# The last layer's second FFN product: its last six input tiles as Strassen blocks in two parts, with low parts made by accumulating transfers

## The chip, the cores and the metric

The kernel runs on one core of a Trainium2 chip. The metric is the device time of one execution in microseconds (us); the figure given for a kernel is the median of its runs.

## The reference, cut to what matters

A two-layer diffusion backbone over 1024 tokens of width 1024, with a 256-token context. The change is in the second product of the second layer's ConvFFN (D_FF = 2816, which is 22 input tiles of 128), which is followed only by the final norm:

```python
def conv_ffn(h, w_up, conv_w, conv_b, w_down, conv_fn):
    g, v = jnp.split(h @ w_up, 2, axis=-1)
    return (jax.nn.silu(conv_fn(g, conv_w, conv_b)) * v) @ w_down
...
        x = x + (gf * conv_ffn(hl, f_w_up[l], f_conv_w[l], f_conv_b[l], f_w_down[l], latent_hconv)).astype(x.dtype)
...
    return rms_norm(x, final_g)
```

## The kernel before

Every fp32 product is made of three fp32r matmuls: an operand is split into a high part (a rounded copy, made by ScalarE, `split`, line 231) and a low part (the operand minus its high part), and `mm` (line 444) adds high·low, low·high and high·high. The low part is made in one of two ways: VectorE subtracts (`split`), or ScalarE writes minus the high part and a DMA that GpSimd issues adds the operand to it from DRAM (`split_dma`, line 238).

`Plan` (line 57) records every operation; `flush` (line 121) sorts them by a list scheduler with costs and due times into one fixed order for each engine. So every instruction has line 165 in the profile. `lag` (line 117) is the delay that the scheduler assumes between engines. SP issues the ordinary DMAs in one queue, in the order of the plan.

`run_units` (line 377) plans the loads. Loads land in four tiles of 128x1024 (`raw`: raw_95, raw_96, raw_97 and raw3) or, for some inputs, in stage tiles (`s`). A landing tile takes its next load when its last reader is done. Weights live in eight slots of 128x512 (`wh`/`wl`, and `wh1`/`wl1`), inputs in 28 slots of 128x512 (`bh0`/`bl0` and `bh`/`bl`).

`ffn` (line 1163) makes gate and value tiles pair by pair. `v_post` (line 1182) multiplies them. For the first 16 of 22 tiles `store_blocks` (line 1200) makes the four input combinations of Strassen's scheme in Winograd's form on VectorE (four subtractions of 128x512) and stores operands and combinations to `bd` (one transfer of 256 KB and three of 512 KB for a pair); the last six are stored plainly to `ad`.

`down` (line 1228) multiplies by `w_down`. The first 16 input tiles come in two groups of eight. A group takes the eight output tiles as four pairs (q = 0 to 3) and makes for each pair seven products (numbered 1 to 7) over 512 columns, each with four input tiles, so 12 matmuls (`down_blocks`, line 1284); each product is added to `x` by VectorE (`scalar_tensor_tensor`, called an evict below). The last six input tiles are plain, in three pieces of columns, 0:512, 512:768 and 768:1024; a piece has eight output tiles of 18 matmuls each. After the evict of each, `residual` (line 1095) squares it on ScalarE and adds the squares into `acct` on VectorE (`norm_sq`, line 462). `final` (line 1371) turns a finished piece's sums into reciprocal roots, spreads them by a matmul, multiplies and stores the output; for pieces 0 and 1 this lies beside the next piece.

Of the kernel before, what the change touches and what calls it, by code (L numbers as in the profile page):

```python
# [13 lines left out]
P = 128  # L14
# [37 lines left out]
class Plan:  # L52
# [131 lines left out]
def hybrid_kernel(ctx: ExitStack, tc: tile.TileContext, out, xs, cs, c, cc, ada, vecs,  # L184
# [88 lines left out]
    bd = dp.tile([P, 7, KD, HALF], F32, tag="bd", name="bd")  # L273
# [32 lines left out]
    def wsrc(key):  # L306
        kind = key[0]
        if kind in ("x", "xc"):
            return wx[key[1]]
        if kind == "g":  # L310
            return wg[key[1]]
        if kind == "o":
            return wo[key[1]]
        if kind == "ri":
            return wri[key[1]]
        if kind == "bo":
            return wbo[key[1]]
        return wdn[key[1], key[2], :, 2 * D:]
# [12 lines left out]
    def weight_item(key):  # L331
        src = wsrc(key)
        n = src.shape[-1]

        def prep(sl, raws):
            hi, lo = flat(sl[0][0], sl[0][2], len(sl))[:, :n], flat(sl[0][1], sl[0][2], len(sl))[:, :n]
            split(hi, lo, raws[0].tile[:, :n], weight_hi[0])
            return hi, lo
        return Item(key, [Raw(src)], -(-n // HALF), prep)

# [121 lines left out]
    def norm_sq(s, m):  # L462
        n = s.stop - s.start
        if m == 0:
            accs[s.start] = acct[:, s.start // HALF, s.start % HALF:s.start % HALF + n]
            act(accs[s.start], x[:, m, s], AF.Square)
        else:
            q = tmp(n)
            act(q, x[:, m, s], AF.Square)
            if s.start >= 768 and m == KD - 1:  # L470
                accs["end"] = q
            else:
                add(accs[s.start], q, accs[s.start], V)
# [621 lines left out]
    def residual(l, sl, m, s, ps, keep):  # L1095
        stt(x[:, m, s], ps, gcol(l, sl, m), x[:, m, s])
        if keep:
            nc.sync.dma_start(xd[:, m, s], x[:, m, s])
        norm_sq(s, m)
# [63 lines left out]
    def ffn(l, second, i):  # L1163
# [18 lines left out]
        def v_post(j0):  # L1182
            done = {0: 0, 1: 0}

            def post(row, h, a, b):
# [7 lines left out]
                if j0 < 16:  # L1193
# [27 lines left out]
    def act_item(key, src, load_after, slots, after, pool="raw"):  # L1221

        def prep(sl, rs):
            for j in (0, 1):
                split(*bslot(slots[j]), rs[0].tile[:, j * HALF:(j + 1) * HALF])
        items[key] = Item(key, [Raw(src, load_after, pool)], 0, prep, after)

    def down(l, ends, i):
# [5 lines left out]
        for g in range(2):  # L1234
# [8 lines left out]
            for q in range(4):  # L1243
                steps = down_blocks(l, g, q, role)
                ends = [unit(f, *(acts[p] if q == 0 else []), k) for p, f, k in steps]
        R = released()
# [5 lines left out]
        last, second = i is None, None  # L1252
        if not last:
            begin, first, second = block_norm(i, R[12:] + R[:12])
        pieces = [H[0], slice(HALF, 768), slice(768, SEQ)] if last else H
        for z, s in enumerate(pieces):
            h, o = s.start // HALF, s.start % HALF
            for m in range(KD):
                def f(w, m=m, h=h, o=o, s=s):
# [5 lines left out]
                    residual(l, 5, m, s, ps, not last)  # L1265
                acts = [("act", l, "t", h, kk) for kk in range(3)] if m == 0 and o == 0 else []
                unit(f, *acts, ("dt", l, m, z))
                if z and last and m == 1:
                    fin = final(pieces[z - 1])
                    call(fin[0])  # L1270
                elif z and last and m == 3:
                    call(fin[1])
                elif z and not last:
                    if m == 0:
                        call(begin)
                    if m == 1:
                        call(norm_cols, i, 1, 0, 1, "norm_mix_g")
                        call(first)
        if last:
            for f in final(pieces[-1]):  # L1280
                call(f)
        return second
# [170 lines left out]
```

## Time and profile before

| | us |
|---|---|
| median of 3 runs | 2081.2 |
| lowest, highest run | 2079.53, 2084.16 |
| profiled execution | 2079.64 |
| its span | 2077.8 |
| VectorE busy in the span | 1640.3 |
| ScalarE busy in the span | 1175.6 |

The profiled execution's own time is 1.84 us above its span and 1.6 us below the median. The stretches of interest: the layer's products with the up weights end near 1850; the last group of Strassen products of `w_down` ends near 1998; the last six input tiles run from there to 2068; the final norm of the last piece follows.

### The profile page before, as it was taken

How to read it: one execution, taken by the hardware profiler on the slowest of the kernel's cores; microseconds unless marked ns; L12 is line 12 of the kernel's file. 1: busy time of each engine (PE TensorE's matmuls, PEld its weight loads, DVE VectorE, ACT ScalarE, POOL GpSimd, SP SyncE). 2: the span in 40 equal slices, each digit the busy share in tenths (PEclk: the TensorE clock that was granted, in tenths of full speed). 3: DMA queues.
4: the chain of work that ended last, by engine and by line, in shares of the span. 5: the costliest groups of instructions: out<-in, count | busy, mean ns of one | idle time of the engine just before them, and what ended most of it. 6: DMA issues, size and time to landing. Idle time of an engine off the chain costs nothing.

```text
span 2077.8 us, 25555 instructions
## 1 busy us (share of the span) xinstructions
PE 2032.1 (98%) x9218; PEld 1679.4 (81%) x9218; DVE 1640.3 (79%) x2408; ACT 1175.6 (57%) x1790; POOL 188.3 (9%) x220
## 2 busy tenths in 40 slices
PE   8899988999999999999999999999999999999998
PEld 6688877788888888878888888888888888878888
DVE  7998999879877787677578977857987776587767
ACT  6266878556655555646356544536655555574445
POOL 0000000010111111111001111001111111111100
PEclk9999999999999999999999999999999999999999
DMA  8644222673677777777465578754566665696655
GB/s 302 192 170 152 71 82 86 205 195 78 174 205 183 191 206 216 204 231 213 117 192 123 155 213 243 229 183 117 136 191 170 185 152 142 168 277 181 157 151 164
DMA packets 134527, 363.72 MB, mean 175 GB/s; under 512 B 13825, under 2 KB 18177, under 8 KB 134273
## 3 DMA queue, kind: packets, MB, share of 16 engines
q1 hardware_dynamic: 103296, 305.46, 44.0%
q0 software_dynamic: 31104, 56.64, 16.7%
q8 instruction: 72, 1.18, 0.2%
q14 instruction: 55, 0.44, 0.1%
HBM read 305.42 MB, written 56.62 MB: 174 GB/s over the span
## 4 chain that ended last, share of the span: by engine, by line
PE 80%; DVE 10%; ACT 4%; DMA 4%; issue 1%; SPq 0%; DVEq 0%; ACTq 0%
PE banks L165 80%; DVE mx L165 2%; ACT mx L165 2%; DMA s<-bd 2%; DVE bl L165 2%; DVE u L165 2%; DVE x L165 2%; DVE wl L165 1%; DMA raw<-in_wdn 1%; ACT bh L165 1%; ACT L165 1%; DVE ul L165 0%; DVE acct L165 0%; DMA x<-in_xs 0%; DVE s L165 0%
## 5 line engine op out<-in xcount | busy, mean ns | idle before, releaser
L165 PE MATMUL banks<-bh,wh 128*128 128x512 f32 (+1 forms) x2720 | 1055.0, 388 | 5.9 <-DVE x L165 2.0
L165 PE MATMUL banks<-bl,wh 128*128 128x512 f32 (+1 forms) x2720 | 1051.2, 386 | 8.8 <-DVE bl L165 8.5
L165 PE MATMUL banks<-bh,wl 128*128 128x512 f32 (+1 forms) x2720 | 1050.5, 386 | 2.1 <-DVE wl L165 2.1
L165 PEld LDWEIGHTS banks<-bl,wh 128*128 128x128 f32 x2720 | 511.8, 188 | 118.7 <-DVE bl L165 15.5
L165 PEld LDWEIGHTS banks<-bh,wh 128*128 128x128 f32 x2720 | 511.7, 188 | 114.5 <-ACT wh L165 3.9
L165 PEld LDWEIGHTS banks<-bh,wl 128*128 128x128 f32 x2720 | 511.6, 188 | 106.4 <-DVE wl L165 4.7
L165 ACT ACTIVATE wh<-raw 128x512 fp32r<-128x512 f32 (+2 forms) x386 | 275.3, 716 | 420.7 <-PE banks L165 369.2
L165 DVE SCALAR_TENSOR_TENSOR x<-banks,mod,x 128x512 f32<-128x512 f32 (+1 forms) x184 | 132.6, 726 | 127.0 <-PE banks L165 126.0
L165 POOL DMA_DIRECT2D wl<-in_wup x132 | 115.0, 871 | 1251.2 <-ACT wl L165 1188.5
L165 ACT ACTIVATE wh<-s 128x512 fp32r<-128x512 f32 x216 | 135.3, 628 | 99.2 <-DVE s L165 70.4
L165 ACT ACTIVATE s<-banks 128x512 f32<-128x512 f32 x174 | 103.5, 596 | 153.9 <-PE banks L165 149.9
L165 DVE TENSOR_TENSOR wl<-raw,wh 128x512 fp32r<-128x512 f32 (+2 forms) x170 | 157.8, 932 | 38.6 <-ACT wh L165 37.2
L165 DVE TENSOR_TENSOR wl<-s,wh 128x512 fp32r<-128x512 f32 x216 | 148.2, 688 | 44.0 <-ACT wh L165 41.5
L165 ACT ACTIVATE wl<-wh 128x512 fp32r<-128x512 f32 x216 | 136.1, 630 | 5.8
L165 DVE TENSOR_TENSOR s<-s,banks 128x512 f32<-128x512 f32 x158 | 107.9, 684 | 31.0 <-PE banks L165 30.6
L165 DVE SCALAR_TENSOR_TENSOR x<-s,vec,x 128x504 f32<-128x504 f32 x132 | 96.6, 741 | 23.4 <-ACT x L165 22.2
L165 DVE TENSOR_TENSOR s<-raw 128x512 f32<-128x512 f32 x72 | 49.6, 689 | 65.0 <-DMA raw<-in_wup 41.9
L165 DVE SCALAR_TENSOR_TENSOR acct<-acct,cb 128x1024 f32<-128x1024 f32 x69 | 84.1, 1219 | 2.1 <-DMA acct<-in_ada 2.1
L165 PE MATMUL banks<-uh,wh 128*128 128x512 f32 (+1 forms) x192 | 70.5, 367 | 8.2 <-ACT mx L165 6.7
L165 PE MATMUL banks<-ul,wh 128*128 128x512 f32 (+1 forms) x192 | 70.1, 365 | 3.1 <-DVE ul L165 3.1
L165 ACT ACTIVATE bh<-s 128x512 fp32r<-128x512 f32 x88 | 51.3, 623 | 37.5 <-DMA s<-bd 33.7
L165 DVE TENSOR_TENSOR bl<-s,bh 128x512 fp32r<-128x512 f32 x88 | 57.3, 687 | 16.1 <-ACT bh L165 16.0
(158 smaller groups left out, 1898.4 us busy)
## 6 DMA issues: line engine op xcount, KB each, us to landing
raw<-in_wup SPq DMA_DIRECT2D x92, 512.0 KB, 4.9
acct<-in_ada SPq DMA_DIRECT2D x69, 512.0 KB, 4.0
wl<-in_wup POOLq DMA_DIRECT2D x132, 256.0 KB, 5.7
bd<-x SPq DMA_DIRECT2D x48, 512.0 KB, 5.3
s<-bd SPq DMA_DIRECT2D x44, 512.0 KB, 5.2
raw<-in_wdn SPq DMA_DIRECT2D x32, 512.0 KB, 5.6
raw<-in_wdn SPq DMA_DIRECT2D x40, 384.0 KB, 3.5
raw<-in_wbi SPq DMA_DIRECT2D x26, 512.0 KB, 5.1
```

Of the source, the lines that this page charges most:

```text
L165: getattr(getattr(self.tc.nc, e), op)(*a, **k)
```

## The change

For the last layer alone, the last six input tiles are made by the same seven products, now over three input tiles each (9 matmuls instead of 12). Layer 0 keeps the plain form (`down_rest`, the old code moved).

- `v_post` also calls `store_blocks` for the last six tiles of the last layer: 12 more subtractions of 128x512 on VectorE, and stores to `bd` instead of `ad`.
- `last_group` makes 20 units of 512 columns (a unit is product and output pair: "10" is product 1 of pair 0) and then, in two pieces of 256 columns, products 5 and 3 of each pair: 8 units of 256 columns each. That is 180 matmuls of 512 columns and 144 of 256, where there were 144 and 288.
- The inputs' low parts (21 tiles) and the low parts of weights 1, 2 and 4 are made by `split_dma`; those of weight products 5, 6, 7 and 3 are made on VectorE from sums and differences of 128x384 (`late_items`). Weights of products 5 and 3 are loaded a second time: 16 loads of 128x768 where there were 24.
- Evicts: one for each product, 20 of 512 columns and 16 of 256 (before, 8 and 16).
- The scheduler's assumed delay after a GpSimd transfer goes from 3.0 to 5.0.

```diff
-        return 0.0 if a == b else 0.95 if a == "sync" else 3.0 if a == "gpsimd" else 1.9 if b == "sync" else 0.2
+        return 0.0 if a == b else 0.95 if a == "sync" else 5.0 if a == "gpsimd" else 1.9 if b == "sync" else 0.2
...
-    bd = dp.tile([P, 7, KD, HALF], F32, tag="bd", name="bd")
+    bd = dp.tile([P, 7, KFF // 2, HALF], F32, tag="bd", name="bd")
...
+    def late_items(name, src1, src2):
+        w = src1.shape[-1] // 2
+        raws = [[Raw(src1), Raw(src2)] for _ in range(2)]
...
+                t = {j: raws[p in (5, 3)][j].tile for j in need[p]}
...
+                if p in (5, 6):
+                    src = s[0] = stmp("w", w)
+                    add(src, a21, a22)
+                    if p == 6:
+                        sub(src, src, a11)
+                elif p == 7:
+                    src = a21
+                    sub(src, a11, a21)
+                elif p == 3:
+                    src = s[0]
+                    sub(src, src, a11)
+                    sub(src, a12, src)
+                else:
+                    split_dma(hi, lo, *{1: (a11, src1[:, :w]), 2: (a12, src1[:, w:]), 4: (a22, src2[:, w:])}[p])
+                    return hi, lo
+                split(hi, lo, src)
...
-                if j0 < 16:
+                if j0 < 16 or l:
...
+                if dma:
+                    split_dma(*bslot(i), t, src[:, j] if len(slots) > 1 else src)
+                else:
+                    split(*bslot(i), t)
...
+    def last_group(l, ends, stored, last_up):
+        role = roles[0]
+        rel = [(j, ends[t]) for t, (_, n) in enumerate(ROLES) for j in role[n]]
+        role3, acts, need = {}, {}, dict(ROLES)
+        for t, p in enumerate((1, 2, 6, 7, 4, 5, 3)):
+            at = rel[3 * t:3 * t + 3]
...
+                act_item(acts[p][e], src, last_up if t < 2 else ends[0] - 8, [j for j, _ in sl], sl[-1][1],
+                         "s" if t < 2 else "raw", True)
...
+        def step(p, q, s):
+            def f(w):
+                n, o = s.stop - s.start, s.start % HALF
+                if p in (1, 5):
+                    st[q, p] = bank()
+                ps = st[q, 5 if p in (3, 5) else 1][:, H[p == 2]][:, :n]
+                for k in range(3):
...
+                r, h = to[p]
+                t = s if p in (5, 3) else H[h]
+                stt(x[:, 2 * q + r, t], ps, gcol(l, 5, 2 * q + r), x[:, 2 * q + r, t])
+                if p in (2, 4, 5, 3):
+                    end(2 * q + r, t)
...
+        for pq in "10 20 60 11 70 21 40 61 12 71 13 41 62 63 72 73 22 23 42 43".split():
+            put(int(pq[0]), int(pq[1]), H[0])
+        pieces = [slice(HALF, 768), slice(768, SEQ)]
+        for z, s in enumerate(pieces):
+            for n, (p, q) in enumerate(((5, 0), (5, 1), (3, 0), (3, 1), (5, 2), (5, 3), (3, 2), (3, 3))):
+                put(p, q, s)
+                if n == 2:
+                    fin = final(pieces[z - 1] if z else H[0])
                     call(fin[0])
...
+                elif n == 4:
+                    call(fin[1])
```

**VectorE, first of the last stage.** These are the rows of the kernel before around the first evicts of the second piece; `x<-banks,mod,x` is an evict, `wl` the low part of a weight, `s<-eye,rt` and `x<-x,banks` the final norm of the piece ahead.

```order
L165 SCALAR_TENSOR_TENSOR x_85<-banks_72,mod_78,x_85 128x256
L165 TENSOR_TENSOR wl_94<-raw_97,wh_93 128x768
L165 SCALAR_TENSOR_TENSOR x_85<-banks_72,mod_78,x_85 128x256
L165 TENSOR_TENSOR wl_94<-raw3_2695,wh_93 128x768
L165 RECIPROCAL rt_84<-rt_84 128x4
L165 TENSOR_TENSOR s_2696<-eye_82,rt_84 128x512
```

One low part or the start of the norm stands between evicts. The changed kernel there, from the second evict of 256 columns (product 5 of pair 1) to the third (product 3 of pair 0); `s` of 128x384 are the weight sums.

```order
L165 SCALAR_TENSOR_TENSOR x_85<-banks_72,mod_78,x_85 128x256
L165 TENSOR_TENSOR wl1_2694<-s_2696,wh1_2693 128x384
L165 TENSOR_TENSOR wl_94<-s_2696,wh_93 128x384
L165 TENSOR_TENSOR s_2696<-raw3_2695 128x384
L165 TENSOR_TENSOR s_2696<-s_2696,raw_95 128x384
L165 RECIPROCAL rt_84<-rt_84 128x4
L165 TENSOR_TENSOR s_2696<-eye_82,rt_84 128x512
L165 TENSOR_TENSOR s_2696<-raw_95,s_2696 128x384
L165 TENSOR_TENSOR wl_94<-s_2696,wh_93 128x384
L165 TENSOR_TENSOR x_85<-x_85,banks_72 128x2x512 x2
L165 SCALAR_TENSOR_TENSOR x_85<-banks_72,mod_78,x_85 128x256
```

Ten operations, two of them 1024 columns wide, now stand between two evicts where one low part stood.

**VectorE, in the 512-column stage.** The kernel before, four evicts after the last group's end (`bl` is the low part of an input):

```order
L165 SCALAR_TENSOR_TENSOR x_85<-banks_72,mod_78,x_85 128x512
L165 TENSOR_TENSOR wl_94<-raw3_2695,wh_93 128x768
L165 SCALAR_TENSOR_TENSOR x_85<-banks_72,mod_78,x_85 128x512
L165 TENSOR_TENSOR wl_94<-raw_95,wh_93 128x768
L165 TENSOR_TENSOR acct_73<-s_2696,acct_73 128x512
L165 TENSOR_TENSOR bl_2692<-raw3_2695,bh_2691 128x512
```

Each evict waits for at most one low part ahead of it. The changed kernel, from the evicts of units 20 and 60 over those of 11, 70 and 21 (the three single ones):

```order
L165 SCALAR_TENSOR_TENSOR x_85<-banks_72,mod_78,x_85 128x512 x2
L165 TENSOR_TENSOR s_2696<-raw_97 128x384
L165 TENSOR_TENSOR s_2696<-s_2696,raw_95 128x384
L165 SCALAR_TENSOR_TENSOR x_85<-banks_72,mod_78,x_85 128x512
L165 TENSOR_TENSOR raw_97<-raw_95,raw_97 128x384
L165 SCALAR_TENSOR_TENSOR x_85<-banks_72,mod_78,x_85 128x512
L165 TENSOR_TENSOR wl1_2694<-s_2696,wh1_2693 128x384
L165 TENSOR_TENSOR wl_94<-raw_97,wh_93 128x384
L165 SCALAR_TENSOR_TENSOR x_85<-banks_72,mod_78,x_85 128x512
L165 TENSOR_TENSOR s_2696<-raw_95 128x384
```

The weight sum of unit 61, which reads raw_97, now stands ahead of the evicts of 11 and 70.

**SP, the landing tiles of that stage.** The kernel before, after its last weights of the Strassen groups:

```order
L165 DMA raw_96<-ad_91 128x2x512
L165 DMA raw_95<-ad_91 128x2x512
L165 DMA raw_97<-ad_91 128x2x512
L165 DMA raw3_2695<-in_wdn 128x768
L165 DMA raw_95<-in_wdn 128x768
L165 DMA raw3_2695<-in_wdn 128x768
L165 DMA raw_96<-in_wdn 128x768
L165 DMA raw_97<-in_wdn 128x768
```

The loads go round the four tiles. The changed kernel in the same place:

```order
L165 DMA raw_97<-bd_92 128x512
L165 DMA raw3_2695<-in_wdn 128x768
L165 DMA s_2696<-bd_92 128x512
L165 DMA raw_97<-bd_92 128x1024
L165 DMA raw_95<-in_wdn 128x768
L165 DMA raw_96<-bd_92 128x512
L165 DMA raw_97<-bd_92 128x512
L165 DMA raw_97<-bd_92 128x1024
L165 DMA raw_96<-in_wdn 128x768
L165 DMA raw_97<-in_wdn 128x768
```

raw_97 takes four loads of inputs one after another, and then the weights that unit 61 needs.

## Rows read from the trace of the kernel before

**Rows 1.** Page, part 1: busy us, share of span, instructions.

```profile
PE 2032.1 (98%) x9218; PEld 1679.4 (81%) x9218; DVE 1640.3 (79%) x2408; ACT 1175.6 (57%) x1790; POOL 188.3 (9%) x220
```

**Rows 2.** Chain of waits, 1940:2078: start us, us, what (xcount).

```profile
1939.81 128.26 PE banks L165 x706
```

**Rows 3.** Stretches: us, then PE, PEld, DVE, ACT, POOL busy; PEclk, DMA share, GB/s.

```profile
1998.30:2031.00 32.70, 32.70 (x147) 27.09 (x146) 20.54 (x29) 18.58 (x28) 0.00 (x0) 1.00 0.46 134
2031.00:2068.00 37.00, 37.00 (x306) 36.47 (x304) 31.41 (x53) 24.35 (x46) 0.00 (x0) 1.00 0.56 178
```

**Rows 4.** Timeline of PE: start us, us, operation, shapes, xcount.

```profile
2010.16 0.39 PE L165 MATMUL banks<-bh,wl 128*128 128x512 f32 x1
2010.39 0.39 PE L165 MATMUL banks<-bh,wh 128*128 128x512 f32 x1
...
2035.10 0.95 PE L165 MATMUL banks<-ones,acct 128*128 128x1 f32 x8
...
2040.29 1.02 PE L165 MATMUL banks<-s,ones 128*128 128x512 f32 x2
...
2062.13 0.28 PE L165 MATMUL banks<-bh,wh 128*128 128x256 f32 x1
2062.25 0.28 PE L165 MATMUL banks<-bl,wh 128*128 128x256 f32 x1
```

**Rows 5.** Timeline of DVE, the last 70 us; in brackets idle before, and its releaser.

```profile
1998.35 0.75 DVE L165 SCALAR_TENSOR_TENSOR x<-banks,mod,x 128x512 f32<-128x512 f32 x1 [1.97 <-PE banks L165]
...
2047.74 0.48 DVE L165 SCALAR_TENSOR_TENSOR x<-banks,mod,x 128x256 f32<-128x256 f32 x1
2048.14 0.42 DVE L165 TENSOR_TENSOR acct<-s,acct 128x256 f32<-128x256 f32 x1
...
2068.09 0.48 DVE L165 SCALAR_TENSOR_TENSOR x<-banks,mod,x 128x256 f32<-128x256 f32 x1 [0.76 <-PE banks L165]
```

**Rows 6.** Groups by line and form, 1998.3:2068: busy us, mean ns, idle before.

```profile
L165 DVE TENSOR_TENSOR acct<-s,acct 128x256 f32<-128x256 f32 x13 | 5.5, 420 | 0.7 <-ACT s L165 0.3
...
L165 DVE TENSOR_TENSOR x<-x,banks 128x1024 f32<-128x1024 f32 x4 | 4.8, 1215 | 0.0
...
L165 ACT ACTIVATE bh<-raw 128x512 fp32r<-128x512 f32 x6 | 3.4, 615 | 0.0
```

**Rows 7.** DMA issues, 1960:2070: KB each, median us from issue to landing.

```profile
raw<-in_wdn SPq DMA_DIRECT2D x24, 384.0 KB, 3.5
raw<-ad SPq DMA_DIRECT2D x4, 512.0 KB, 3.8
```

**Rows 8.** DMA issues, 1700:1960.

```profile
raw<-bd SPq DMA_DIRECT2D x6, 512.0 KB, 5.1
bd<-x SPq DMA_DIRECT2D x1, 256.0 KB, 5.2
```

**Rows 9.** What PE waited for, 1830:1870: us, times, longest.

```profile
PE banks L165 <- DVE bl L165: 0.9, 1, 0.9
PE banks L165 <- DVE x L165: 0.8, 1, 0.8
```

**Rows 10.** Timeline of DVE at the turn from up to down products.

```profile
1847.18 1.29 DVE L165 TENSOR_TENSOR bl<-s,bh 128x512 fp32r<-128x512 f32 x2 [1.04 <-ACT bh L165]
...
1857.83 1.29 DVE L165 TENSOR_TENSOR bl<-s,bh 128x512 fp32r<-128x512 f32 x2 [1.35 <-ACT bh L165]
```

**Rows 11.** Timeline of PE in layer 0: idle before the first row in brackets.

```profile
9.43 1.66 PE L165 MATMUL banks<-uh,bh 128*128 128x512 f32 x6 [2.97 <-ACT bh L165]
...
355.02 0.79 PE L165 MATMUL banks<-uh,wh 128*128 128x512 f32 x1 [5.47 <-ACT mx L165]
355.61 0.63 PE L165 MATMUL banks<-ul,wh 128*128 128x512 f32 x1
356.04 0.63 PE L165 MATMUL banks<-uh,wl 128*128 128x512 f32 x1
```

**Rows 12.** A stretch in layer 0, columns as in rows 3.

```profile
352.00:359.00 7.00, 3.98 (x9) 3.13 (x10) 6.93 (x6) 6.97 (x9) 0.00 (x0) 0.54 0.00 0
```

More of the change, by code (lines that the diff above doesn't have):

```diff
@@ L460, in hybrid_kernel, with norm_sq @@
     accs = {}
-    def norm_sq(s, m):
+    def norm_sq(s, m, first, end=False):
         n = s.stop - s.start
-        if m == 0:
+        if first:
             accs[s.start] = acct[:, s.start // HALF, s.start % HALF:s.start % HALF + n]
@@ L469, in norm_sq @@
             act(q, x[:, m, s], AF.Square)
-            if s.start >= 768 and m == KD - 1:
+            if end:
                 accs["end"] = q
@@ L1219, in ffn, with act_item @@
         return down(l, ends, i)
[L1221 removed]
+    def act_item(key, src, load_after, slots, after, pool="raw", dma=False):
         def prep(sl, rs):
[L1224 to L1225 removed]
+            for j, i in enumerate(slots):
+                t = rs[0].tile[:, j * HALF:(j + 1) * HALF]
+                if dma:
+                    split_dma(*bslot(i), t, src[:, j] if len(slots) > 1 else src)
+                else:
+                    split(*bslot(i), t)
         items[key] = Item(key, [Raw(src, load_after, pool)], 0, prep, after)
@@ L1245, in down, with down_rest @@
                 ends = [unit(f, *(acts[p] if q == 0 else []), k) for p, f, k in steps]
+        if i is not None:
+            return down_rest(l, ends, i)
+        last_group(l, ends, stored, last_up)
+    def down_rest(l, ends, i):
         R = released()
@@ L1251, in down @@
                          ends[(sl + 1) // 4])
[L1252 to L1256, printed above, removed]
+        begin, first, second = block_norm(i, R[12:] + R[:12])
+        for z, s in enumerate(H):
             h, o = s.start // HALF, s.start % HALF
@@ L1264, in f @@
                         mm(ps, w, slice(k * P, (k + 1) * P), rh[:, o:o + n], rl[:, o:o + n], k == 0, k == 5)
-                    residual(l, 5, m, s, ps, not last)
+                    residual(l, 5, m, s, ps, True)
                 acts = [("act", l, "t", h, kk) for kk in range(3)] if m == 0 and o == 0 else []
                 unit(f, *acts, ("dt", l, m, z))
-                if z and last and m == 1:
-                    fin = final(pieces[z - 1])
+                if z and m == 0:
+                    call(begin)
@@ L1270, in down @@
                     call(fin[0])
-                elif z and last and m == 3:
+                elif n == 4:
                     call(fin[1])
[L1273 to L1282, printed above, removed]
+        for f in final(pieces[-1]):
+            call(f)
```

40 lines of the change are left out of this document (38 added, 2 removed).

## The prediction

> **What bounds the kernel now.** I read the shares of the page first: PE is busy 98% of the span, VectorE (DVE) 79% [rows 1]. Then the chain of waits over the end: from 1939.81 the set end is one unbroken run of 128.26 us of matmuls up to 2068.07 [rows 2], so at that place a matmul less is time less, as long as nobody else becomes late. Then the stretches after the last Strassen group: in the 512-column stage PE works all 32.70 us and DVE 20.54; in the two 256-column pieces PE works all 37.00 and DVE 31.41, ScalarE 24.35 [rows 3]. The reader is to see that DVE has 12 us of slack in the first of these stretches and under 6 in the second, and that the change gives DVE work in both and takes PE's time away. The last evict stands at 2068.09; what follows (square, sums, root, spread, multiply, store) is the same in both kernels, 9.7 us to the span's end.
>
> **The matmuls removed.** Pitch, from start to start, is .23 us for 512 columns (2010.16 to 2010.39; .2267 on the mean of many) and .12 for 256 [rows 4]. Before: 144 x .2267 + 288 x .1195 = 67.1 us. After: 180 x .2267 + 144 x .1195 = 58.0. PE's saving is 9.1 us. The last group's end is seen in DVE's evict at 1998.35 [rows 5]. With PE alone, 20 units of 9 matmuls (2.04 each) and one of 256 columns (1.075) bring the first 256-column evict (product 5 of pair 0) to 1998.35 + 40.8 + 1.1 = 2040.2; 15 more units (16.1) and the norm's matmuls of pieces 0 and 1 (.95 + 1.02 us for the first [rows 4], about half for the second: 2.7) would bring the last evict to 2059.05, 9.0 earlier than before.
>
> **What DVE must do in the last stage.** By the order of the changed kernel, from that first evict to the last DVE has 15 evicts of 256 columns, 13 sums, differences and low parts of weights of 384, 2 additions into acct of 512 and 12 of 256, 4 multiplications of 1024 and 2 of 512, two roots and two spreads. A DVE operation back to back costs .08 less than its duration (an evict of .48 at 2047.74, the next start at 2048.14: .40 [rows 5]); one that reads what the one ahead has just written costs its duration and about .1. So: 15 x .40 = 6.0; 13 x .55 = 7.2 (no row has 384 columns; between .42 for 256 [rows 6] and .69 for 512 (two in 1.29 [rows 10]), dependent and independent ones mixed; bounds 13 x .47 = 6.1 and 13 x .65 = 8.5); 12 x .33 = 4.0 and 2 x .6 = 1.2 from the acct row's .42 [rows 6]; 4 x 1.13 = 4.5 from the 1.215 row [rows 6]; 2 x .6 = 1.2; roots and spreads 1.6. Sum 25.7, with some 1 us of waits for ScalarE's high parts and squares in between: 26.8. DVE's last evict is then at 2040.2 + 26.8 = 2067.0, not at 2059. PE pauses instead: in the order the two multiplications of 1024 and five weight operations stand between two evicts, and the weights of products 5 and 3 of the later pairs are made only as slots come free, so I expect one PE pause near 2 us ahead of product 3 of pair 1 and one near 4 us ahead of product 3 of pair 2. Of 9.1 us gained, **this stage keeps 1.2** (bounds from the 384-column price and the waits: 0 to 3.5).
>
> **New waits in the 512-column stage.** The order shows raw_97 taking four loads of inputs, then the weights that the sum of unit 61 reads; that sum stands on DVE ahead of the evicts of units 11 and 70. A unit of the last group is 12 x .2267 = 2.7 us; the input slot of the first of these loads comes free when the third of its seven units ends, at 1998.2 - 4 x 2.7 = 1987.3. From there each load waits for ScalarE's reading of the one ahead (.6 us a tile [rows 6], and the low copies between, as long): .6, then 512 KB landing in 3.8 [rows 7] and four ScalarE operations and a weight's two, 3.6; 256 KB, which I put at 3.0, and .6; 512 KB in 3.8 and three operations, 1.8; and the weights' 384 KB in 3.5 [rows 7]; with .3 for the issue each time that is 21.9, so 2009.2. Sum, difference and evict bring 70's evict to 2012.1; PE is done with 10, 20, 60, 11, 70 and 21 at 2010.4, and unit 40, which goes into the bank half that 70's evict empties, waits 1.65. The next loads into the tiles just freed repeat this at 40's and 61's evicts: another 1.4 ahead of 71. If the landings go as those of bd at the turn, 5.1 [rows 8], it is 5. I take **2.8**, bounds 0 and 5: below, since the 12 us of DVE's slack would hide it if ScalarE went ahead with the input tiles.
>
> **The turn from up to down products.** Twelve more subtractions and their stores come in; those of the first two pairs (8 x .6 = 4.8 us of DVE) lie under up products, where nothing waits for them: nothing. The last pair's four stand at the turn, where PE already waits .9 for a low part of an input and .8 for an x [rows 9]. They cost 4 x .6 = 2.4, a multiplication comes in beside them (.6), and the first must wait for the store of its operand to land (256 KB in 5.2 [rows 8]); against that DVE has gaps of 1.04 and 1.35 there [rows 10], and a pair of convolution steps (1.5) moves ahead. I take **1.4**, bounds .5 and 3.5. With the cover of those gaps gone it would be the full 3.0.
>
> **The rest.** 33 accumulating transfers are issued by GpSimd, which is idle in both last stretches [rows 3]: nothing. The lag of 5 in the scheduler moves single operations in earlier stretches, on DVE, ScalarE and POOL; layer 0's matmuls keep their order: 0, bounds -2 and 2. Eight weight loads less: nothing, SP has room.
>
> **Sum.** -1.2 + 2.8 + 1.4 = +3.0. The profiled execution took 2079.64 (span 2077.8), which is 1.6 below the median of 2081.2. So the span goes to 2080.8, the profiled time to 2082.6, and against the median I say **2084.2**.
>
> **Rivals.** (1) DVE doesn't bind the last stage: its sums run at the lower price and PE's pauses stay short, so that 6 to 8 of the 9.1 us stand, and the 512-stage hides its loads. For it: 12 us of DVE slack; against: 26.8 us of fixed DVE order for 18.8 of PE. 2081.2 - 9.1 + 1.9 = 2074. Chance .12. (2) Slower: the one-tile chain of loads starves the 512-stage. It decides from landings of 4.5 us and above; at 5.1 the four later landings come 4 x 1.4 = 5.6 later, of which the 1.4 ahead of 71 and the 1.65 ahead of 40 each grow by some 2: 2084.2 + 4.2 = 2088.4. For it: the bd row of 5.1; against: DMA share is .46 and .56 at the end [rows 3]. Chance .20. (3) The clock falls in the last stage. Before 355.02 PE stood 5.47 us; afterwards its 512-column matmuls start .43 apart (355.61 to 356.04), and the stretch was granted .54, the lower of its two levels, 1.2 against 2.4 GHz. After 2.97 us at 9.43 six took 1.66, the higher level [rows 11, 12]. A pause near 4 us lies between. Nine matmuls at the low pitch cost 9 x .2 = 1.8: 2086.0. Chance .16. The Trainium skill, "TensorE: Matmul & The Clock Gate", section "Why this matters for your kernels", says that a long idle gap between bursts puts TensorE back to half rate; this would put the pause of 4 us on the falling side, and the sum to 2086.0, while the row at 9.43 leaves it open. (4) The lag reorders an earlier stretch so that a wait there grows or goes: +-2, 2082 or 2086. Chance .06. The change does what it says; the plan's order shows the units.
>
> **How the numbers follow.** My forecast has .46: within 2080 to 2086.5. No change here means within 0.2%, 4.2 us, about what a measurement of this kernel can tell: 2077.0 to 2085.4. Forecast: .02 faster, .37 same, .07 slower. Rival 1: .11 faster, .01 same. Rival 2: .02 same, .18 slower. Rival 3: .07 same, .09 slower. Rival 4: .04 same, .02 slower. Together faster .13, same .51, slower .36. The range of 8 in 10 leaves out most of rival 1 and the far end of rival 2: 2077.0 to 2089.5.
>
> **What would show it.** Right: 144 x 256 and 180 x 512 matmuls after 1998; PE pauses of 2 and 4 us in the last stage put down to DVE, with DVE above 93% from the first 256-column evict to the last; about 27 us between these two; PE pauses ahead of 40 and 71 that end on an evict held by a weight sum; a turn 1.4 longer. Wrong: the last evict within 20 us of the first of 256 columns; no PE pause before it; a granted clock under 1.00 at 2045 to 2065.

## The result

The changed kernel takes 2109.9 us (median of 4 runs, 2106.9 to 2115.7), the kernel before in the same comparison 2082.1 (4 runs): a ratio of 1.0137, 95% interval 1.0112 to 1.0162. The prediction was 2084.2 with a range of 2077.0 to 2089.5: wrong, by 25.7 us, and outside the range. The page of the changed kernel, parts 1 and 4, where [rows 1, 2] stood:

```profile
span 2105.1 us, 25486 instructions
PE 2035.9 (97%) x9110; PEld 1673.7 (80%) x9110; DVE 1645.8 (78%) x2436; ACT 1190.6 (57%) x1836; POOL 217.0 (10%) x253
...
PE 76%; DVE 8%; issue 6%; DMA 4%; ACT 3%; POOL 1%; SPq 0%; POOLq 0%; DVEq 0%; ACTq 0%
```

The span is 27.3 us longer. To see where, I cut it at five marks that both traces have: the first and the 32nd evict of the last layer's down product, the end of its last Strassen group (the last seen evict of that group's 2.72 us rhythm, plus one or more such steps), the first matmul of 256 columns, and the last evict. The marks of the changed kernel, from its timelines of DVE and PE (start, duration, operation), of which the one at 2002.59 stands one step of 2.72 before the group's end at 2005.31:

```profile
1846.26 0.75 DVE L165 SCALAR_TENSOR_TENSOR x<-banks,mod,x 128x512 f32<-128x512 f32 x1
...
1951.15 0.74 DVE L165 SCALAR_TENSOR_TENSOR x<-banks,mod,x 128x512 f32<-128x512 f32 x1
...
2002.59 0.75 DVE L165 SCALAR_TENSOR_TENSOR x<-banks,mod,x 128x512 f32<-128x512 f32 x1 [1.97 <-PE banks L165]
...
2094.72 0.48 DVE L165 SCALAR_TENSOR_TENSOR x<-banks,mod,x 128x256 f32<-128x256 f32 x1
```

```profile
2063.47 0.28 PE L165 MATMUL banks<-bh,wh 128*128 128x256 f32 x1
```

In the kernel before the same marks stand at 1845.39, 1943.99, 1998.35 [rows 5], 2030.79 and 2068.09 [rows 5]:

```profile
1845.39 0.74 DVE L165 SCALAR_TENSOR_TENSOR x<-banks,mod,x 128x512 f32<-128x512 f32 x1
...
1943.99 0.75 DVE L165 SCALAR_TENSOR_TENSOR x<-banks,mod,x 128x512 f32<-128x512 f32 x1
```

```profile
2030.79 0.28 PE L165 MATMUL banks<-bh,wh 128*128 128x256 f32 x1
```

In the changed one they stand at 1846.26, 1951.15, 2005.31, 2063.47 and 2094.72. The predicted column is the prediction's own sum, put at these marks: 40.8 + 2.8 for the fourth line, and from 2039.15 (its first 256-column matmul without waits) to 2067.0 for the fifth.

| stretch | before | predicted | changed kernel |
|---|---|---|---|
| start to first down evict | 1845.4 | 1845.4 | 1846.3 |
| to the 32nd evict (the turn) | 98.6 | 100.0 | 104.9 |
| to the end of the last group | 54.4 | 54.4 | 54.2 |
| to the first 256-column matmul (512-column stage) | 32.4 | 43.6 | 58.2 |
| to the last evict (last stage) | 37.3 | 27.9 | 31.3 |
| to the span's end | 9.7 | 9.7 | 10.4 |

So of the 24 us by which the span was missed, 14.6 lie in the 512-column stage, 4.9 in the turn, 3.4 in the last stage. What PE waited for in the first of these (us, times, longest):

```profile
PE banks L165 <- DMA bl<-bd: 8.8, 8, 2.2
PE banks L165 <- DMA wl<-in_wdn: 1.8, 1, 1.8
```

All 10.6 us are waits for low parts that GpSimd's transfers add, which the prediction had priced at nothing. The stages by stretch (columns as in [rows 3]):

```profile
2005.30:2063.50 58.20, 47.66 (x181) 35.77 (x180) 28.33 (x48) 31.31 (x60) 20.02 (x23) 0.91 0.91 205
2063.50:2094.70 31.20, 23.54 (x161) 21.04 (x159) 26.71 (x55) 18.23 (x40) 0.88 (x1) 0.95 0.42 131
2012.00:2020.00 8.00, 5.72 (x16) 3.82 (x15) 1.82 (x4) 4.79 (x10) 2.99 (x4) 0.79 1.00 228
2034.00:2041.00 7.00, 7.00 (x20) 5.56 (x21) 1.69 (x3) 1.05 (x2) 0.87 (x1) 0.63 0.36 53
```

The reader is to see two things. DVE is busy 28.33 of 58.20: it isn't what binds there. And the granted clock is .91 over the stage, .63 in 2034 to 2041 where PE works without a break: of the 17.4 us above the 40.8 that 180 matmuls of 512 columns need, 10.6 are waits; some 4.2 are matmuls at the lower level after them, which start .43 apart instead of .23; the rest lies beside the nine pauses, where a matmul doesn't overlap with the next. One low part's way, from ScalarE's copy (the first of the two) over GpSimd's issue to PE (three timelines, matched by the kernel's order of copies and adds):

```profile
1999.31 1.14 ACT L165 ACTIVATE bl<-bh 128x512 fp32r<-128x512 f32 x2
```

```profile
2006.08 0.89 POOL L165 DMA_DIRECT2D bl<-bd  x1 [1.18 <-ACT wh L165]
```

```profile
2013.89 0.50 PE L165 MATMUL banks<-bl,wh 128*128 128x512 f32 x1 [1.69 <-DMA bl<-bd]
```

And the transfers of that time in the changed kernel (KB each, median us to landing), beside [rows 7]:

```profile
raw<-in_wdn SPq DMA_DIRECT2D x16, 384.0 KB, 6.0
bl<-bd POOLq DMA_DIRECT2D x21, 256.0 KB, 6.9
```

The copy is made at 1999.9, its add is issued only at 2006.1, and PE starts at 2013.9: 14 us, where a subtraction on DVE is a .69 row behind the copy. Plain loads take 6.0 instead of 3.5.

### The profile page after: what moved, and what is told of

It is laid out like the page before. It is cut to its first block, busy times and chain, and to the rows that moved or that the text cites. A ratio compares the mean times of both kernels' runs of the same rounds, so it can differ in the third digit from the quotient of the medians.

```text
span 2105.1 us, 25486 instructions
## 1 busy us (share of the span) xinstructions
PE 2035.9 (97%) x9110; PEld 1673.7 (80%) x9110; DVE 1645.8 (78%) x2436; ACT 1190.6 (57%) x1836; POOL 217.0 (10%) x253
## 3 DMA queue, kind: packets, MB, share of 16 engines
HBM read 312.50 MB, written 58.98 MB: 176 GB/s over the span
## 4 chain that ended last, share of the span: by engine, by line
PE 76%; DVE 8%; issue 6%; DMA 4%; ACT 3%; POOL 1%; SPq 0%; POOLq 0%; DVEq 0%; ACTq 0%
PE banks L165 76%; DMA s<-bd 2%; DVE mx L165 2%; ACT mx L165 2%; DVE u L165 2%; DVE x L165 1%; DVE bl L165 1%; ACT bh L165 1%; POOL bl L165 1%; POOL wl L165 1%; DVE acct L165 1%; DVE wl L165 1%; DVE ul L165 1%; DMA bl<-bd 1%; ACT L165 0%
## 5 line engine op out<-in xcount | busy, mean ns | idle before, releaser
L165 PEld LDWEIGHTS banks<-bl,wh 128*128 128x128 f32 x2684 | 506.4, 189 | 136.6 <-DVE bl L165 17.6
L165 ACT ACTIVATE wh<-raw 128x512 fp32r<-128x512 f32 (+3 forms) x378 | 263.4, 699 | 393.2 <-PE banks L165 340.8
L165 DVE SCALAR_TENSOR_TENSOR x<-banks,mod,x 128x512 f32<-128x512 f32 (+1 forms) x196 | 141.3, 727 | 133.0 <-PE banks L165 132.0
L165 ACT ACTIVATE wh<-s 128x512 fp32r<-128x512 f32 (+1 forms) x228 | 141.6, 622 | 112.2 <-DVE s L165 86.5
L165 DVE TENSOR_TENSOR wl<-s,wh 128x512 fp32r<-128x512 f32 (+1 forms) x228 | 154.6, 680 | 38.0 <-ACT wh L165 35.1
L165 DVE TENSOR_TENSOR wl<-raw,wh 128x512 fp32r<-128x512 f32 (+3 forms) x150 | 137.6, 920 | 34.0 <-ACT wh L165 32.5
L165 ACT ACTIVATE wl<-wh 128x512 fp32r<-128x512 f32 (+1 forms) x228 | 142.3, 625 | 6.2
L165 DVE TENSOR_TENSOR s<-s,banks 128x512 f32<-128x512 f32 x158 | 107.7, 684 | 27.8 <-PE banks L165 27.3
L165 DVE SCALAR_TENSOR_TENSOR x<-s,vec,x 128x504 f32<-128x504 f32 x132 | 96.5, 741 | 24.0 <-ACT x L165 22.8
L165 DVE TENSOR_TENSOR s<-raw 128x512 f32<-128x512 f32 (+1 forms) x80 | 54.0, 675 | 70.7 <-DMA raw<-in_wup 42.8
L165 POOL DMA_DIRECT2D wl<-in_wdn x60 | 52.2, 870 | 303.1 <-ACT wl L165 288.5
L165 DVE TENSOR_TENSOR x<-x 128x512 f32<-128x512 f32 x100 | 68.6, 688 | 11.7 <-DMA bd<-x 10.5
```

The costliest lines, as they stand in the source:

```text
L165: getattr(getattr(self.tc.nc, e), op)(*a, **k)
```

## The experiments

Each kernel is given by its edit, its expectation as it was written before the run, and what came. The table has the stretches of its profile (turn, 512-column stage, last stage, as above); the ratio is that of the kernel to the kernel before.

| kernel | median | ratio, 95% interval | turn | 512 | last |
|---|---|---|---|---|---|
| before | 2082.1 | | 98.6 | 32.4 | 37.3 |
| changed | 2109.9 | 1.0137, 1.0112 to 1.0162 | 104.9 | 58.2 | 31.3 |
| e1 own tensor | 2112.7 | 1.0139, 1.0108 to 1.0171 | 107.8 | 57.8 | 32.6 |
| e2 inputs on DVE | 2096.6 | 1.0064, 1.0045 to 1.0083 | 106.2 | 41.6 | 32.8 |
| e3 weights on DVE | 2102.1 | 1.0092, 1.0072 to 1.0113 | 105.8 | 45.2 | 34.4 |
| e4 both on DVE | 2093.4 | 1.0049, 1.0035 to 1.0063 | 106.3 | 40.6 | 32.6 |
| e5 stores by GpSimd | 2098.4 | 1.0087, 1.0072 to 1.0103 | 112.3 | 40.6 | 34.9 |
| e6 no subtractions | 2094.4 | 1.0066, 1.0046 to 1.0086 | 105.8 | 40.6 | 32.5 |
| e7 no multiplications | 2086.6 | 1.0026, 1.0011 to 1.0040 | 105.1 | 40.6 | 28.6 |
| e8 before, 12 adds | 2081.4 | 1.0005, .9996 to 1.0015 | 98.5 | 32.4 | 37.3 |
| e9 order of pairs | 2090.8 | 1.0039, 1.0025 to 1.0053 | 101.9 | 40.6 | 34.3 |
| e10 lag 8 | 2109.2 | 1.0135, 1.0107 to 1.0163 | 103.8 | 58.1 | 34.1 |
| e11 squares on PE | 2094.2 | 1.0055, 1.0033 to 1.0076 | 104.4 | 41.7 | 37.6 |
| e12 nine on DVE | 2098.9 | 1.0082, 1.0067 to 1.0097 | 103.6 | 42.2 | 39.0 |
| e13 late reload | 2088.7 | 1.0027, 1.0016 to 1.0037 | 100.0 | 40.6 | 34.8 |

In e3 PE waited .6 us within the last group, so its group ends at 2010.3 and not at the 2009.5 of the rhythm. Kernels with the same code in a stretch differ by up to 2.7 us in it (the turn of e4 and e12, of e9 and e11), so smaller steps are not read. The 62.8 us in the first expectations is to the second evict of 256 columns, a slip; to the first matmul of 256 columns, as in the table, it is 58.2.

**The added low parts: e2, e3, e4.** From here on "e4's base" is the changed kernel with both edits.

```diff
 act_item(..., sl[-1][1], "s" if t < 2 else "raw",
-         True)                                      # e2, e4
+         False)
...
-                    split_dma(hi, lo, *{1: (a11, src1[:, :w]), 2: (a12, src1[:, w:]), 4: (a22, src2[:, w:])}[p])
-                    return hi, lo
+                    src = {1: a11, 2: a12, 4: a22}[p]   # e3, e4
```

> The changed kernel with one edit: the low parts of the 21 input tiles are subtracted by VectorE again, not added by GpSimd's transfers. From the end of the last Strassen group to the first evict of 256 columns the changed kernel took 62.8 us where its matmuls need 41.9. Theory A (PE waits for transfers that GpSimd issues: 10.5 us for input low parts, which land 6.9 us after they are issued): the stretch shrinks by 10 us or more, to 50 to 53, PE's wait for these transfers is gone, and the time falls to 2098 to 2101. Theory B (the loads that follow one another through one landing tile set the stretch, however the low part is made): it stays above 58 and the time above 2105.

> The changed kernel with one edit: the low parts of the plain weight operands (products 1, 2 and 4 of the six last tiles, 12 of 128x384) are subtracted by VectorE, and the inputs' low parts stay with GpSimd's transfers. Theory A: the wait of 1.8 us for a weight goes, and with 12 of 33 transfers less the inputs' land somewhat sooner (6 us instead of 6.9): the stretch before the first 256-column evict goes from 62.8 to 57 to 60 and the time to 2105 to 2108. Theory B: VectorE's 12 operations of .55 us come on top or are hidden: 62 to 66, time 2109 to 2114.

> Both edits: no low part of the last six input tiles or of their weights is added by a transfer; VectorE makes all 33. Theory A: the stretch before the first 256-column evict falls to 46 to 52 us (the remaining excess over 41.9 is the landing of loads and VectorE's order), raw tiles land in 3.5 to 4 us again instead of 6.0, the clock stays at 1.00 between 2005 and 2041, and the time is 2094 to 2100. Theory B: 57 to 63 and 2105 to 2112. Neither gives less than before's 2082, since the turn (6 us) and the last stage (26.6 us for 18.8 of matmuls) stay.

e2's stage went from 58.2 to 41.6, e4's to 40.6, which is 180 matmuls without a pause. Theory B falls: the loads through one landing tile are the same in all three, and cost nothing. e4's row for its stage (columns as in [rows 3]), with DVE at 34.21 of 40.60 and the clock at 1.00:

```profile
2006.80:2047.40 40.60, 40.60 (x180) 33.62 (x180) 34.21 (x59) 19.82 (x36) 0.00 (x0) 1.00 0.49 149
```

e3 went further than theory A had it: with all 21 inputs added and only the weights' 12 adds gone, the stage is 45.2, and what PE still waits for in it is DVE, not a transfer:

```profile
PE banks L165 <- DVE x L165: 3.8, 3, 1.7
```

So the landing time of an add isn't the cause by itself; e3's adds land as late as before:

```profile
bl<-bd POOLq DMA_DIRECT2D x21, 256.0 KB, 6.5
```

**Twelve adds in the kernel before: e8.** One part of the change alone.

```diff
+                if dma:
+                    split_dma(*bslot(slots[j]), t, src[:, j])
...
-                         ends[(sl + 1) // 4])
+                         ends[(sl + 1) // 4], "raw", i is None)
```

> The kernel before with one part of the change alone: the low parts of the last six input tiles (12 of 128x512, plain products) are added by GpSimd's transfers. Its own stretch from the end of the last Strassen group to the first matmul of 256 columns is 32.4 us, without a pause. Theory A (a low part added by a transfer is ready 7 to 8 us after ScalarE's copies, where VectorE's is ready after .7): it grows by 6 to 10 us, with PE's waits put down to that transfer, and the time goes to 2088 to 2092. Theory A' (the waits of the changed kernel come from many adds, of inputs and weights, behind one another in GpSimd's one queue): with 12 adds alone and none of weights beside them it stays within 3 us, 2081 to 2085.

2081.4 us, a ratio of 1.0005 (.9996 to 1.0015): no difference that can be measured, and no wait of PE in the stage. The adds land no sooner, beside plain loads of 512 KB that take 3.7 (transfers of e8, KB each, median us to landing):

```profile
bl<-ad POOLq DMA_DIRECT2D x12, 256.0 KB, 6.7
raw<-ad SPq DMA_DIRECT2D x4, 512.0 KB, 3.7
```

A landing of 6.7 us is hidden where the add is issued early enough. Theory A', many adds behind one another, is left.

**Is it order, load or margin: e10, e12.**

```diff
-        return ... else 5.0 if a == "gpsimd" else ...
+        return ... else 8.0 if a == "gpsimd" else ...    # e10
...
-                         "s" if t < 2 else "raw", True)
+                         "s" if t < 2 else "raw", t not in (2, 3, 4))   # e12
```

> The changed kernel with one number changed: the scheduler assumes 8.0 us, not 5.0, from the issue of a GpSimd transfer to its use, about what the profile shows (6.9 us landing and .9 of issue). All 33 added low parts stay. Theory A (what an added low part costs is its landing and its load on the DMA engines): the stretch from the last group's end to the first matmul of 256 columns stays at 53 to 60 us (58.2 in the changed kernel, 40.8 without a pause). Theory G (it is the order: transfers for inputs queued in GpSimd behind those for weights whose slot isn't free, and ScalarE's copies made in an order that assumed they would be ready sooner): it falls to 42 to 50, and the time to 2093 to 2102.

> The changed kernel with VectorE making the low parts of 9 of the 21 input tiles, those of products 6, 7 and 4, which are loaded into the four common landing tiles and needed in the 512-column stage; the other 12 (products 1, 2, 5 and 3) and the 12 of weights stay with added transfers. Theory M (margin: an input slot comes free at most some 19 us before its product, and load, ScalarE's two copies, turn in GpSimd's queue and the add's landing of 6.9 us one after another use that up; 24 adds as such cost nothing, as 12 did in the kernel before): the stretch from the last group's end to the first matmul of 256 columns falls from 58.2 to 41 to 45 us, time 2093 to 2098. Theory A (every add loads the DMA engines, which were busy all through the stretch): with 24 of 33 adds left it falls by a fourth of the 17.4 us at most, to 52 to 56, time 2104 or more.

e10 stayed at 58.1: a better guess of the delay alone doesn't help the scheduler. It doesn't settle theory G, since it left the adds in GpSimd's queue in the order of the changed kernel (the same run of bl and wl rows in both timelines). e12 came to 42.2, in theory M's 41 to 45, with 24 of 33 adds left. The load on DMA is still there, and costs nothing here (e12):

```profile
raw<-in_wdn SPq DMA_DIRECT2D x15, 384.0 KB, 6.3
bl<-bd POOLq DMA_DIRECT2D x12, 256.0 KB, 6.6
```

What e2, e3 and e12 have in common is fewer adds in GpSimd's queue while the low parts of this stage pass through it. That queue is on the chain of waits that ended last, from 1993 until the last input of the stage has landed (changed kernel; start, duration):

```profile
1996.20 5.26 issue
2001.51 0.85 POOL bl L165
...
2028.15 5.73 DMA bl<-bd
2033.93 9.09 PE banks L165 x28
```

This last add goes out 22.8 us after the last group's end (2005.3); in e3, with 21 adds, it goes out 11.6 us after it (2010.3). Its copy had been ready since 2008.9:

```profile
2008.30 0.62 ACT L165 ACTIVATE bl<-bh 128x512 fp32r<-128x512 f32 x1
```

So ScalarE, which the profile names for some of GpSimd's waits, isn't what they wait for. Three starts of PE, each at the landing of an add, and GpSimd's queue around them show what it is:

```profile
2011.24 0.50 PE L165 MATMUL banks<-bl,wh 128*128 128x512 f32 x1 [1.67 <-DMA bl<-bd]
...
2013.89 0.50 PE L165 MATMUL banks<-bl,wh 128*128 128x512 f32 x1 [1.69 <-DMA bl<-bd]
...
2015.32 0.80 PE L165 MATMUL banks<-bl,wh 128*128 128x512 f32 x1 [0.46 <-DMA bl<-bd]
```

```profile
2004.03 0.86 POOL L165 DMA_DIRECT2D bl<-bd  x1 [0.18 <-issue]
2006.08 0.89 POOL L165 DMA_DIRECT2D bl<-bd  x1 [1.18 <-ACT wh L165]
2008.17 0.87 POOL L165 DMA_DIRECT2D bl<-bd  x1 [1.20 <-ACT wh L165]
2011.51 0.86 POOL L165 DMA_DIRECT2D wl<-in_wdn  x1 [2.46 <-issue]
2014.16 0.86 POOL L165 DMA_DIRECT2D bl<-bd  x1 [1.79 <-ACT bl L165]
2015.59 1.81 POOL L165 DMA_DIRECT2D bl<-bd  x2 [0.57 <-ACT wh L165]
```

PE's start at 2011.24 is the landing of the add of 2004.03, and GpSimd issues its next add but two at 2011.51; the landings of 2006.08 and 2008.17 and the issues at 2014.16 and 2015.59 follow in the same way. By the landings that the traces hold, none of the 3373 transfers that GpSimd issued in the fifteen traces (from each one's fourth on) went out sooner than .31 us after the third one before it had landed, and 129 went out just then: 28 in the changed kernel, 16 in e3, 12 in e12, 7 in e8, one in e2. So three of its transfers are under way at a time, and no more. From 2001.48 to 2034.19 the changed kernel's 17 issues each waited for that, one in 2.04 us.

This tells how much is lost, and where. The seventh unit, 40, is the last to need new inputs: all 15 and five weights, 20 adds. An estimate: from the first of these issues (1986.85) 19 steps of 2.04 us and a landing of 5.7 lead to 2031.3, and the last in fact landed at 2033.9. PE without waits would have come to unit 40 at 2005.3 + 6 x 2.04 = 2017.5, so 16 us sooner; 17.4 were lost. For the same unit e12 needs 11 adds, by the same sum 26 us, and e2 five, which the 30.7 us from 1986.85 to 2017.5 hold; in e3 it is 15, whose last landed at 2027.1, while PE, held by DVE, came to that unit at 2026.9. The weights' adds stand ahead of inputs in the one queue, but no run put the same 33 in another order. The scheduler gives a GpSimd transfer 1.2 us of its queue (`cost`, line 102), and e10 changed only the delay behind it.

**The turn: e1, e5, e6, e9, e13.** In the changed kernel SP issues the first stage loads of the down product (s<-bd) at 1844.26; before, three go at 1839.36. What SP's queue waited for at the turn of the changed kernel:

```profile
SPq L165 <- DMA bd<-x: 10.6, 1, 10.6
SPq L165 <- DVE bl L165: 8.1, 5, 1.9
```

In the plan (`record`) a store of two combinations covers, as a range of addresses, all pairs between the two, so loads of other pairs count as depending on it. e1 gives the last six tiles a tensor of their own; e5 takes the last pair's stores off SP's queue; e6 leaves the four subtractions out.

```diff
+    bt = dp.tile([P, 7, 3, HALF], F32, tag="bt", name="bt")
...
+            t, q = (bt, q - 8) if q >= 8 else (bd, q)       # e1, e9, e13
...
-                nc.sync.dma_start(bd[:, i:i + 2, q], ...)
+                (G if q == 10 else nc.sync).dma_start(bd[:, i:i + 2, q], ...)   # e5, on e4's base
...
+            if q < 10:                                       # e6, on e4's base
                 sub(b11, b12, b11)
...
+            qs = (3, 0, 1, 2) if i is None and g == 0 else (0, 1, 2, 3)   # e9, on e1 and e4's base
```

> The changed kernel with one edit: the combinations of the last layer's last six tiles go to a DRAM tensor of their own, so that no load of the first groups can be taken to depend on their stores. Theory C (the turn from up to down products became 6.0 us longer because loads of the first Strassen group wait in SP's queue for the late stores to land): the last Strassen group ends 4 to 5 us earlier than the changed kernel's 2005.3, near 2000.5, and SP's wait of 12.7 us for a store is gone; the time falls by as much, to about 2105. Theory D (it is VectorE's four subtractions at the turn): nothing changes, the group ends at 2004 to 2006 and the time stays near 2110. The last 100 us are untouched under both.

> The kernel without added low parts, with one edit: the four stores of the last pair's combinations at the turn are issued by GpSimd and not by SP. From the first evict of the down product to the 32nd, the kernel before took 98.6 us and that without added low parts 106.3. Theory Q (SP's queue: the loads of the first group's inputs stand behind stores whose data VectorE has not made yet, and so begin late): the stretch falls to 99 to 102 and the time by 4 to 7, to 2086 to 2089. Theory D (VectorE's own four subtractions and what waits for them): 105 to 107, time as without the edit, 2093.

> The kernel without added low parts, with the last pair's four subtractions left out (part of the combinations is then plain operands). Theory D: the stretch from the first to the 32nd evict of the down product falls from 106.3 to about 103 or less, at least the 2.4 us of the four. Theory Q: the stores then wait for nothing but the multiplications, so it falls too, to 102 to 104; if it falls to 99 as before, the subtractions and the stores' wait for them are the whole of the turn; if it stays above 105, it is neither but the amount of stores (1.75 MB) or the reloads of x behind them.

> The kernel without added low parts, with the combinations of the six last tiles in a DRAM tensor of their own, and the pair of outputs 6, 7 taken first in the last layer's first Strassen group (order 3, 0, 1, 2). Theory E (the turn's 6 to 8 us are two things: loads that were held behind the late stores because their places in one tensor overlap as ranges, and, once that is undone, the reload of x tiles 4 and 5, which must wait for the last pair's stores to land; PE waited 4.5 us for it with an own tensor alone): both are gone, the stretch from the first to the 32nd evict returns to 98 to 101 us from 106.3, the last group ends at 1998 to 2001 and the time falls to 2085 to 2088. Theory F (the 2.6 MB more of stores and the subtractions themselves load DMA and VectorE): it stays above 104 and the time above 2090. The later stages stay at 40.6 and 32.6 us, so the kernel stays slower than before's 2081 in both.

e1's time did not fall, but its trace shows both halves of the matter. The loads are early again, and the eleven waits of PE between 1850 and 1870 are down to two as before; in their place stands one. SP's timeline of e1, and PE's:

```profile
1839.21 3.48 SPq L165 DMA_DIRECT2D s<-bd  x3
...
1876.13 0.36 SPq L165 DMA_DIRECT2D bt<-x  x1
1882.24 0.33 SPq L165 DMA_DIRECT2D x<-xd  x1
```

```profile
1892.84 0.77 PE L165 MATMUL banks<-bh,wh 128*128 128x512 f32 x1 [4.53 <-DVE x L165]
```

Behind this wait the granted clock fell to the lower level for 6.8 us (e1, columns as in [rows 3]), which is part of why the turn didn't shorten:

```profile
1891.90:1898.70 6.80, 5.86 (x14) 4.64 (x15) 5.60 (x10) 1.84 (x4) 0.86 (x1) 0.50 0.28 44
```

The x tile that held the last pair can be reloaded only when its store has landed, and its evict waits for that. e5 was worse, 112.3: the stores then stand in GpSimd's queue, and SP waits longer than before for DVE to free its stage tiles. e6 stayed at 105.8: the subtractions are not it, and theory D falls. Theory Q's forecast failed too, but e5 left the loads' dependence on the stores in place, so it doesn't say what an earlier load would give. The 2.6 MB of stores in theory F are 2.36 by the pages (58.98 MB written against 56.62). e9, which needs that x tile last, came to 101.9, and its trace shows SP standing 8 us at the reload, with weight loads behind it:

```profile
1883.80 0.39 SPq L165 DMA_DIRECT2D bt<-x  x1
1891.79 0.33 SPq L165 DMA_DIRECT2D x<-xd  x1
1892.22 6.58 SPq L165 DMA_DIRECT2D raw<-in_wdn  x4
```

e13 places the reload behind those loads (and, for the last stage, adds the low parts of six late inputs by transfers).

```diff
+                def late():
+                    for m in (4, 5):
+                        load_res(m)
+                        nc.ops[-1][5].add(nc.last_mm)
...
-                         "s" if t < 2 else "raw", False)
+                         "s" if t < 2 else "raw", t > 4)
```

> The kernel with the own tensor, the order 3, 0, 1, 2 and no added low parts, with two edits: the reloads of x tiles 4 and 5 are placed in SP's queue behind the weights of the third pair (with the order 3, 0, 1, 2 alone SP stood 8.0 us on the landing of a store, with weight loads behind it, and VectorE waited 4.1 us for weights), and the low parts of the six input tiles of products 5 and 3, needed last, are added by transfers again (6 VectorE operations of .6 leave the last stage). Theory E: the turn falls from 101.9 to 98.5 to 99.5 us; theory V: the last stage from 34.3 to 30 to 32 us. Together the time falls from 2090.8 to 2083 to 2086; slower than before's 2081 still. If the turn stays at 102, the queue behind the reload wasn't the rest of it.

The turn is 100.0, so 4.9 of the changed kernel's 6.3 us are explained by two chains in SP's queue: loads behind stores that they count as depending on, and reloads of x behind the landing of late stores. The step from e9 to e13, 1.9, is too small to be read by itself, and so are the 1.4 left. The time, 2088.7, is not the 2083 to 2086 expected: the last stage did not shorten.

**The last stage: e7, e11.**

```diff
+                if s.start:                                  # e7, on e4's base
                     mul(x[:, m:m + w, s], x[:, m:m + w, s], rs.unsqueeze(1).to_broadcast([P, w, n]))
...
+                    T.matmul(ptile[:, 3, j:j + 1], q[:, j * P:(j + 1) * P], ones[:, 0:1], start=n == 1, ...)   # e11, on e9
```

> The kernel without added low parts, with the first piece's four multiplications of 128x1024 by the norm's factor left out (it is stored unscaled). From the first matmul of 256 columns to the last evict that kernel took 32.6 us, where PE needs about 20. Theory V (VectorE sets the last stage by its own work): 4.5 us of its work go, and the stretch falls to 28 to 29. Theory W (it is the weights of products 5 and 3, made only as their slots come free): the stretch stays at 31 to 33.

> The kernel with the own tensor and the order 3, 0, 1, 2, without added low parts, and with the squares of the two 256-column pieces summed over tokens by TensorE into a PSUM bank of their own, so that 12 additions of 128x256 leave VectorE (12 x .33 = 4.0 us) and 32 one-column matmuls (.12 each, 3.8 us) come to TensorE, which stands idle for some 12 us there. Theory V (VectorE sets the last stage): the stretch from the first matmul of 256 columns to the last evict falls from 32.6 to 28 to 30 us and the time to 2080 to 2084, level with the kernel before. Theory W (weights and slots set it): 32 to 34, time as for the kernel without this edit.

In e11 the two columns accumulate by turns in one bank and the factors of these pieces come out as other numbers; its times alone are read. e7 shortened the last stage by 4.0, from 32.6 to 28.6, for 4.5 us of DVE work, at nearly the same granted clock (.90 over the stage in e4, .88 in e7): theory V. In the changed kernel the place is the one that the prediction named, the evict behind two multiplications of 1024:

```profile
2077.88 0.36 PE L165 MATMUL banks<-bh,wh 128*128 128x256 f32 x1 [2.93 <-DVE x L165]
```

e11 took 4 us of work from DVE and became slower there, 37.6. One of its stretches, with PE busy from end to end:

```profile
2066.00:2075.00 9.00, 9.00 (x56) 9.00 (x56) 3.53 (x7) 4.09 (x10) 0.00 (x0) 0.66 0.23 86
```

DVE is busy 3.53 of 9.00: here TensorE at the lower level sets the pace. So e11 does not contradict theory V, nor does it support it: with DVE lighter the bound went to a slower PE. e12 (39.0) and e13 (34.8) show the same in part; e13's stretch 2050 to 2060 was granted .67.

No version beat the kernel before. The best of the changed ones, e7 left aside, is e13, at 1.0027 (1.0016 to 1.0037) of its time.

## Why the prediction was wrong

- **The matmuls removed**: right. e4 runs its 20 units in 40.6 us, the prediction's 40.8. (The norm's matmuls, 2.7 us in it, come to 3.0 by its own rows; the forecast doesn't rest on them.)
- **The rest, "33 accumulating transfers are issued by GpSimd, which is idle: nothing"**: the step that failed. With the adds the 512-column stage is 58.2, without them 40.6 (e4): 17.6 us, where nothing was put. GpSimd being idle before says nothing of how long each add takes until PE may read it (6.9 us where the subtraction took .69), nor of how many its queue can have under way: three, so that one went out every 2.04 us, and the 20 that the seventh unit needs came 16 us late. The prediction's rows had no add at all; the trace of before has adds for weights near this place, from which it could have bounded the landing:

```profile
wl<-in_wdn POOLq DMA_DIRECT2D x3, 256.0 KB, 4.9
```

  That a landing alone would not have told the loss is shown by e8, where twelve adds are free.
- **New waits in the 512-column stage, 2.8 us from one landing tile**: wrong mechanism. e4 has the same four loads through raw_97 and no wait. Landings like those of bd at the turn (5.1 us) did come in the changed kernel: its loads of 384 KB took 6.0, and 3.5 in e4, without the adds.
- **The last stage**: DVE binds it, as said, and e7 shows it. From the first 256-column matmul to the last evict 27.9 were predicted and 31.3 came. The sum of DVE's work was right: 25.7, and it was busy 25.2 of the 29.7 us from the first 256-column evict to the last. Its waits were mis-sized, at 1 us for 4.5. In the same stage PE waited 1.8 us for added low parts, priced at nothing, and the clock fell after the pauses, which the prediction had only as a rival of 1.8 us (.95 over the stage).
- **The turn, 1.4 us**: mis-sized, 6.3 came. The subtractions that made up the price cost nothing that e6 could find; the stores in SP's queue did, which the prediction had only as one landing of 5.2 us (SP waited 10.6 us there for one).
- **Rivals**: the slower one (landing tiles) had the right sign and place and the wrong cause; the clock rival happened in addition, not instead, and mostly in the 512-column stage. The Trainium skill ("TensorE: Matmul & The Clock Gate", section "Why this matters for your kernels") says that a long idle gap puts TensorE back to half rate. The trace shows the fall, but the pauses ahead of it were short: at most 2.2 us each in the 512-column stage of the changed kernel.

## What to carry to other kernels

An operation moved to an idle engine isn't free: price it by the time from its inputs to the moment its reader may start, by what stands ahead of it in that engine's one queue, and by how many that queue can have under way; then compare the number needed in a stage with the number that it can issue in that time. Ask of each in-order DMA queue which entry waits for something late (a store whose data isn't made, a reload behind a store) and what is queued behind it. Where matmuls are saved by work on another engine, compare that engine's sum in the same stage first: here 9.1 us of matmuls were exchanged for a stage that DVE sets.

## What the runs showed of the hardware

An add by GpSimd's transfer of 256 KB landed in 6.5 to 7.3 us (median) in every kernel that had one for inputs, also in e8, with few transfers beside it, where plain loads of 512 KB took 3.7. GpSimd had at most three transfers under way in all fifteen traces: its next one went out .31 us after a landing at the soonest. Plain loads of 384 KB beside 21 or more adds took 5.8 to 6.5 instead of 3.5; beside the 12 of e2 they took 3.7, of e8 4.1. TensorE's granted clock fell after pauses well below the 5.47 us of [rows 11]: in e9 after three of .65, .83 and .57 us between 2043 and 2047, to .54 in the next stretch, while PE was busy in 6.98 of 7.00 us of it:

```profile
2039.90:2047.00 7.10, 4.87 (x32) 3.96 (x30) 7.10 (x15) 4.42 (x9) 0.00 (x0) 0.97 0.30 64
2047.00:2054.00 7.00, 6.98 (x28) 5.87 (x28) 4.64 (x11) 5.02 (x10) 0.00 (x0) 0.54 0.27 105
```

The length of a pause alone doesn't tell: at the same place of layer 0 a single pause of 2.97 us left the higher level in [rows 11], and one of 1.96 us in e12 was followed by the lower, six matmuls taking 2.58 us instead of 1.66 and the granted clock reading .50 from 9.80 to 13.20:

```profile
9.39 2.58 PE L165 MATMUL banks<-uh,bh 128*128 128x512 f32 x6 [1.96 <-ACT bh L165]
```

Short waits can cost more in clock than in waiting: the three of e9 make 2.05 us, and the stretch behind them ran 7.00 us at .54, by an estimate .46 x 7.00 = 3.2 us less of full-speed work.
